# Stick-breaking attention: a third score bank, the scans' second operand and the column sums in one bank, filling output products in row order

## The chip, the cores and the metric

One core of one Trainium2 chip runs the kernel. The metric is the device time of one execution in microseconds (us), as the median of several executions. The engines are named as the profile names them: PE is TensorE (PEld its weight loads), DVE is VectorE, ACT is ScalarE, POOL is GpSimd and SP is SyncE, which issues most DMAs.

## What is computed

A decoder trunk of two layers on 1024 tokens with 1024 features. Layer 0 mixes tokens by a gated linear recurrence, layer 1 by stick-breaking attention with 16 heads of 64; a SwiGLU block follows each. The change lies in the attention alone. With z the scaled scores of a block of 128 queries against the keys up to them:

```python
strict = s_idx < t_idx
log_fail = jnp.where(strict, jax.nn.log_sigmoid(-z), 0.0)
suffix = lax.cumsum(log_fail, axis=3, reverse=True) - log_fail
weights = jnp.where(strict, jnp.exp(jax.nn.log_sigmoid(z) + suffix), 0.0)
outs.append(jnp.einsum("bhqk,bhkd->bhqd", weights.astype(vb.dtype), vb))
```

So a key's weight is its own sigmoid times the products of sigmoid(-z) over all keys between it and the query. Then the heads' outputs are multiplied by `attn_w_o` and added to the residual.

## The kernel before

**Products in 16-bit parts.** Most fp32 products are made as three fp16 products (`mm3`, lines 157 to 159: high x high, high x low, low x high). Rows in the profile with line 157, 158 or 159 are these.

**Pairs and chunks.** The 16 heads are worked in eight pairs q = 0 to 7 (`LAST` is 7). For each head, `chunk_list` gives twelve chunks of scores: eight with the diagonal (128 to 512 keys) and four more of 512 keys to their left for the later query blocks. A chunk passes through four steps:

- `z_part` (lines 2118, 2119): two TensorE products write the scores to a PSUM bank `z_ps`, from a pool `psZ` with two banks that are taken in turn.
- `z_rest` (line 2156): ScalarE takes the sigmoid of -z into SBUF (`w`; `wp`, `wd`, `wt` in the last pair).
- `scan` (lines 2164, 2167): a VectorE scan runs over the keys backwards and multiplies the sigmoids up. Its second operand holds 2^15 at the diagonal place and zeros elsewhere: it is fp32 in PSUM (`units_ps`), and for the last pair bfloat16 in SBUF (`unit`, read backwards). The scan of a left chunk starts from the first column of the diagonal chunk's result.
- `turn_weights` (lines 2179, 2180, 2189): ScalarE and GpSimd split the result into two fp16 parts, and a DMA transposes them. In the last pair TensorE transposes instead (`t_part`, line 2199), and ScalarE and VectorE split (`t_split`, lines 2208, 2209).

`av_part` (line 2231) multiplies the transposed weights with the differences of the values, eight to ten steps after the scores.

**PSUM.** Eight banks: two each for `psZ` (scores), `psT`, `psO` (weighted sums) and `psQ` (projections). Of `psT`, one bank holds `units_ps` until the last pair; the other serves `n_ps` of pair 0 and then stands unused until the last pair's transposes.

**Column sums.** For each pair, `column_norms` sums the squares of the value weights' columns: ScalarE squares them (`sq`, line 1968), eight one-column products form the sums on TensorE (`n_ps`, line 1950), and VectorE makes a power of two of them (lines 1956, 1958). For pairs 1 to 7, `n_ps` takes a bank of `psZ` in turn. `sums` is run by `due()`, which stands at the start of a step, before the step's `z_part`.

**The order.** All five engines keep the order in which the program is written (a manual schedule). The loop over `u` is the step: `due()`, then one chunk's `z_part` and `z_rest`, its `scan`, the previous chunk's `turn_weights`, one task from the list `later`, two filling projections (`fill`: six products for the next pair's q, k or v), and `av_part`. Semaphores are placed by the framework from the tiles that instructions touch.

**Filling output products.** In the last two heads there are no projections left, and `out_fill` starts the output projection: 21 rows of `mm3`, seven for each of three output tiles, at steps set by `amount`. Row k needs `xl[k]`, the heads of pair k; row 6 of each was third in order. `xl[6]` is written by lines 2255 and 2256 some steps after pair 6 is done.

**Set-up.** `unit` is made by GpSimd (lines 1913, 1914), and ScalarE casts it into `units_ps` (line 1916).

Of the kernel before, what the change touches and what calls it, by code (L numbers as in the profile page):

```python
# [8 lines left out]
F32 = mybir.dt.float32  # L9
F32R = mybir.dt.float32r  # L10
BF16 = mybir.dt.bfloat16
F16 = mybir.dt.float16
I32 = mybir.dt.int32
# [5 lines left out]
P = 128  # L19
S = 1024  # L20
D = 1024
ND = D // P
NT = S // P
NB = 512
# [11 lines left out]
def trunk(  # L36
# [21 lines left out]
    nc = tc.nc  # L58
# [33 lines left out]
    ident = cp.tile([P, P], F32, name="ident")  # L92
# [63 lines left out]
    def mm3(ps, wh, wl, mh, ml, first, last, **kw):  # L156
        nc.tensor.matmul(ps, lhsT=wh, rhs=mh, start=first, stop=False, **kw)  # L157
        nc.tensor.matmul(ps, lhsT=wh, rhs=ml, start=False, stop=False, **kw)  # L158
        nc.tensor.matmul(ps, lhsT=wl, rhs=mh, start=False, stop=last, **kw)  # L159

    def pair16(t):
        t = t.bitcast(F16)
        n = t.shape[-1] // 2
        return t[:, 0:n], t[:, n : 2 * n]
# [135 lines left out]
    with ExitStack() as st, tc.manual_schedule(engines={E.PE, E.Activation, E.DVE, E.Pool, E.SP}):  # L300
# [49 lines left out]
        ps = pst("vps0")  # L350
# [71 lines left out]
        for r0, r1 in ((0, 32), (32, 64), (64, P)):  # L422
            ps = pst("vps")
# [1475 lines left out]
    UP = 2.0**15  # L1899

    pos, obs, begun = ExitStack(), ExitStack(), {}
    with ExitStack() as st:
# [3 lines left out]
        psZ = pos.enter_context(tc.tile_pool(name="psZ", bufs=2, space=PSUM, side="right", reuse_waits="tile"))  # L1906
        psT = st.enter_context(tc.tile_pool(name="psT", bufs=2, space=PSUM, reuse_waits="tile"))
# [2 lines left out]


        unit = ap.tile([P, NB], BF16, name="unit")
        nc.gpsimd.memset(unit[:, 0 : NB - P], 0.0)
        nc.gpsimd.tensor_scalar_mul(unit[:, NB - P :], ident, UP)
        units_ps = psT.tile([P, NB], F32, tag="T", name="units")
        nc.scalar.copy(units_ps, unit[:, ::-1])
        g2 = ap.tile([P, ND], BF16, name="g2")
        nc.scalar.square(g2, vc[:, V_MIX + ND : V_MIX + 2 * ND])
        zz = ap.tile([P, NT], F32, name="zz")
# [12 lines left out]
        def stage(task, steps=1):  # L1932
            soon.append([steps, task])
# [8 lines left out]
        def column_norms(raw, q):  # L1942
            sq = ap.tile([P, ND, P], BF16, tag="vx", name="sq", bufs=2)
            r3 = raw.rearrange("p (k c) -> p k c", k=ND)

            def sums():
                pool, tag = (psZ, "z") if q else (psT, "T")
                n_ps = pool.tile([P, NB], F32, tag=tag, name="n_ps")[:, 0:1]
                for k in range(ND):
                    nc.tensor.matmul(  # L1950
                        n_ps, lhsT=sq[:, k], rhs=g2[:, k : k + 1], start=k == 0, stop=k == ND - 1
                    )

                n2, h = (ap.tile([P, 1], t, tag=x, name=x, bufs=2) for x, t in (("n2", F32), ("nh", I32)))
                sv[q], av_[q] = (ap.tile([P, 1], I32, tag=x, name=x, bufs=3) for x in ("sv", "av"))
                nc.vector.tensor_scalar(n2, n_ps, 1e-30, 2.0, op0=ALU.max, op1=ALU.mult)
                one = float(1 << 23)
                nc.vector.tensor_single_scalar(h, n2.bitcast(I32), 24, op=ALU.logical_shift_right)

                def factors():  # L1960
                    nc.gpsimd.tensor_scalar(sv[q], h, -one, 213 * one, op0=ALU.mult, op1=ALU.add)
                    nc.gpsimd.tensor_scalar(av_[q], h, one, 41 * one, op0=ALU.mult, op1=ALU.add)
                    nc.gpsimd.tensor_add(K_N, K_N, n2)
                    nc.gpsimd.tensor_mul(f32(av_[q]), f32(av_[q]), O_UP)

                stage(factors)

            squared = lambda i: nc.scalar.square(sq[:, 4 * i : 4 * i + 4], r3[:, 4 * i : 4 * i + 4])

            def second():  # L1970
                squared(1)
                stage(sums, 2)

            return lambda: squared(0), second
# [138 lines left out]

        def z_part(q, hx, j, ci, c0, c1, diag):
            nk = (j + 1) * P
            ps = psZ.tile([P, NB], F32, tag="z", name="z_ps")
            lhsT = Q[q][hx][:, j * P : (j + 1) * P]
            nc.tensor.matmul(ps[:, 0 : c1 - c0], lhsT=lhsT, rhs=KK[q][hx][:, 0, c0:c1], start=True, stop=False)
            nc.tensor.matmul(ps[:, 0 : c1 - c0], lhsT=lhsT, rhs=KK[q][hx][:, 1, c0:c1], start=False, stop=True)  # L2119
            return ps  # L2120
# [7 lines left out]
        LAST = NP - 1  # L2128
# [29 lines left out]
        def scan(q, hx, j, ci, c0, c1, diag):  # L2158
            F = W[q, hx, j, ci]
            n = min(c1, (j + 1) * P) - c0  # L2160
            rev = F[:, ::-1]
            add = unit[:, NB - n :][:, ::-1] if q == LAST else units_ps[:, 0:n]
            if diag:
                nc.vector.tensor_tensor_scan(rev, rev, add, 0.0, op0=ALU.mult, op1=ALU.add)  # L2164
            else:
                first = W[q, hx, j, 1][:, 0:1]
                nc.vector.tensor_tensor_scan(rev, rev, add, first, op0=ALU.mult, op1=ALU.bypass)

        T = {}
# [21 lines left out]
        def unit_list(q, hx):  # L2191
            kbs = ((0, 1, 2, 3), (4, 5, 6, 7, 0, 1, 2, 3))
            return [(q, hx, G, kb, kb == 4 * G, kb == 3) for G in range(2) for kb in kbs[G]]
# [70 lines left out]
        units = [u for q, hx in heads for u in unit_list(q, hx)]  # L2264
# [9 lines left out]
        def out_fill():  # L2274
            qs.close()
            po = obs.enter_context(tc.tile_pool(name="fp0", bufs=1, space=PSUM, side="right", reuse_waits="tile"))
            for x, n in ((0, 0), (0, 1), (1, 1)):
                d = mix[0].order[x]
                w = mix[0].w[d]
                if x:  # L2280
                    assert c >= len(chunks)
                    ps = psZ.tile([P, NB], F32, tag="z", name="ob_ps")
                else:
                    ps = po.tile([P, NB], F32, name=f"ob{n}")
                begun[d, n] = ps
                for k in (0, 1, 6, 2, 3, 4, 5):
                    mm3(ps, w[0][:, k], w[1][:, k], *pair16(xl[k][n]), k == 0, False)
                    yield

# [2 lines left out]
        with tc.manual_schedule(engines={E.PE, E.Activation, E.DVE, E.Pool, E.SP}):  # L2292
# [30 lines left out]
            gains = [len(units) - x for x in (31, 29, 27)]  # L2323

            last_two, out_work = len(units) - 2 * 12, out_fill()
            amount = {x: 2 for x in (9, 10, 11, 12)}
            amount.update({x: 1 for x in (*range(-5, 1), *range(14, 21))})
# [6 lines left out]
            for u in range(-LEAD, len(units)):  # L2334
# [6 lines left out]
                for a in some:  # L2341
                    z_rest(z_part(*a), *a)
# [5 lines left out]
                for a in some:  # L2348
                    scan(*a)
# [13 lines left out]
                if u in gains:  # L2363
                    z_rest(z_part(*chunks[c]), *chunks[c])
                    scan(*chunks[c])
                    turning.append(chunks[c])
                    c += 1
# [52 lines left out]
```

## Time and profile before

| | |
|---|---|
| median of 3 runs | 2058.79 us (2058.74 to 2060.89) |
| profiled execution | 2058.67 us, its span 2056.2 us |
| PE busy | 2008.2 us (98%) |
| DVE busy | 1778.6 us (86%) |
| ACT busy | 1451.3 us (71%) |
| POOL busy | 297.6 us (14%) |
| granted TensorE clock | 1.00 |
| first and last score product | 972.0 and 1342.0 us |

The span runs from the first to the last instruction; the execution's time is 2.5 us longer. Times in rows are counted from the span's start. A row of the timeline gives start, duration, engine, line, operation, the tile written and the tiles read, the shape and the count; in brackets, the idle time of the engine just before and what ended it. A row of a list of waits gives who waited for whom, the total in us, how often and the longest. TensorE's products overlap: the next one starts some 0.22 us after one of 512 columns began, though each lasts 0.38.

### The profile page before, as it was taken

How to read it: one execution, taken by the hardware profiler on the slowest of the kernel's cores; microseconds unless marked ns; L12 is line 12 of the kernel's file. 1: busy time of each engine (PE TensorE's matmuls, PEld its weight loads, DVE VectorE, ACT ScalarE, POOL GpSimd, SP SyncE). 2: the span in 40 equal slices, each digit the busy share in tenths (PEclk: the TensorE clock that was granted, in tenths of full speed). 3: DMA queues.
4: the chain of work that ended last, by engine and by line, in shares of the span. 5: the costliest groups of instructions: out<-in, count | busy, mean ns of one | idle time of the engine just before them, and what ended most of it. 6: DMA issues, size and time to landing. Idle time of an engine off the chain costs nothing. (4 is left out here: it accounts for less than half of the span.)

```text
span 2056.2 us, 28572 instructions
## 1 busy us (share of the span) xinstructions
PE 2008.2 (98%) x10059; PEld 1095.0 (53%) x10059; DVE 1778.6 (86%) x2639; ACT 1451.3 (71%) x2280; POOL 297.6 (14%) x327
## 2 busy tenths in 40 slices
PE   8999999999999999999999999899999999999998
PEld 7888885454555444444545445454445555444445
DVE  6887888989999899897888877878899999999886
ACT  6777546777777677766888888854768777665566
POOL 1000010000000000001666666412000000000002
PEclk9999999999999999999999999999999999999999
DMA  7232471564555797523888887554355556674412
GB/s 257 62 93 62 147 242 62 159 213 161 179 176 188 247 298 223 161 90 93 151 157 154 147 152 155 116 177 152 114 178 186 168 164 214 211 258 146 134 42 92
DMA packets 443999, 328.07 MB, mean 160 GB/s; under 512 B 165832, under 2 KB 365648, under 8 KB 443856
## 3 DMA queue, kind: packets, MB, share of 16 engines
q1 hardware_dynamic: 443696, 325.99, 55.0%
q8 instruction: 78, 1.28, 0.3%
q14 instruction: 65, 0.53, 0.1%
q10 hardware_dynamic: 160, 0.27, 0.0%
HBM read 215.55 MB, written 69.21 MB: 138 GB/s over the span
## 5 line engine op out<-in xcount | busy, mean ns | idle before, releaser
L159 PE MATMUL p_ps<-v,wb 128*128 128x512 f16 x524 | 198.7, 379 | 3.8 <-DVE wb L785 3.4
L159 PE MATMUL p_ps<-v,wc 128*128 128x512 f16 x524 | 198.6, 379 | 3.2 <-DVE wc L785 3.2
L157 PE MATMUL p_ps<-v,wb 128*128 128x512 f16 x524 | 198.5, 379 | 2.9 <-ACT ta L1487 0.8
L158 PE MATMUL p_ps<-v,wc 128*128 128x512 f16 x524 | 198.6, 379 | 0.0
L158 PE MATMUL p_ps<-v,wb 128*128 128x512 f16 x524 | 198.6, 379 | 0.0
L157 PE MATMUL p_ps<-v,wc 128*128 128x512 f16 x524 | 198.5, 379 | 0.0
L2180 POOL TENSOR_TENSOR wx<-w,wx 128x512 f16<-128x512 f32 (+1 forms) x140 | 153.1, 1095 | 119.8 <-ACT wx L2179 85.6
L159 PE MATMUL p_ps<-v,wa 128*128 128x512 f16 x396 | 150.1, 379 | 0.0
L158 PE MATMUL p_ps<-v,wa 128*128 128x512 f16 x396 | 150.1, 379 | 0.0
L157 PE MATMUL p_ps<-v,wa 128*128 128x512 f16 x396 | 150.0, 379 | 0.0
L780 ACT ACTIVATE wb<-sb,fac 128x1024 f16<-128x1024 f32 x44 | 50.5, 1148 | 110.4 <-DVE sb L800 110.4
L2164 DVE TENSOR_TENSOR_SCAN w<-w,units 128x128 f32<-128x128 f32 (+1 forms) x112 | 91.3, 815 | 39.7 <-ACT w L2156 39.6
L245 POOL TENSOR_TENSOR acc<-acc,rbc 128x512 f32<-128x512 f32 x30 | 39.6, 1321 | 495.9 <-ACT rbc L244 495.8
L157 PE MATMUL p_ps<-v,wd 128*128 128x512 f16 x254 | 96.2, 379 | 8.3 <-ACT G L1487 4.7
L2156 ACT ACTIVATE w<-z_ps,zz 128x512 f32<-128x512 f32 (+2 forms) x168 | 95.5, 576 | 8.6 <-PE z_ps L2119 6.9
L158 PE MATMUL qk_ps<-rh,w 128*128 128x512 f16 x264 | 100.0, 379 | 0.3 <-DVE rh L251 0.3
L159 PE MATMUL qk_ps<-rh,w 128*128 128x512 f16 x264 | 100.0, 379 | 0.0
L157 PE MATMUL qk_ps<-rh,w 128*128 128x512 f16 x264 | 100.0, 379 | 0.0
L157 PE MATMUL a_ps<-xh,whi 128*128 128x512 f32 x248 | 97.1, 391 | 0.0
L159 PE MATMUL p_ps<-v,wd 128*128 128x512 f16 x254 | 96.3, 379 | 0.8 <-DVE wd L785 0.8
L2179 ACT CAST wx<-w 128x512 f16<-128x512 f32 (+1 forms) x140 | 79.8, 570 | 24.4 <-DVE w L2164 13.2
L158 PE MATMUL a_ps<-xl,whi 128*128 128x512 f32 x248 | 96.6, 390 | 0.1
(493 smaller groups left out, 5621.5 us busy)
## 6 DMA issues: line engine op xcount, KB each, us to landing
raw<-in_ffn_w_in SPq DMA_DIRECT2D x80, 512.0 KB, 4.3
pd<-U SPq DMA_DIRECT2D x90, 256.0 KB, 2.4
loose<-in_ffn_w_out SPq DMA_DIRECT2D x44, 512.0 KB, 3.7
raw<-pd SPq DMA_DIRECT2D x66, 256.0 KB, 3.6
row<-pd SPq DMA_DIRECT2D x62, 256.0 KB, 4.5
raw<-in_ffn_w_out SPq DMA_DIRECT2D x56, 256.0 KB, 3.8
raw<-in_attn_w_qkv SPq DMA_DIRECT2D x24, 512.0 KB, 4.2
raw<-in_lru_w_out SPq DMA_DIRECT2D x16, 512.0 KB, 3.6
```

Of the source, the lines that this page charges most:

```text
L157: nc.tensor.matmul(ps, lhsT=wh, rhs=mh, start=first, stop=False, **kw)
L158: nc.tensor.matmul(ps, lhsT=wh, rhs=ml, start=False, stop=False, **kw)
L159: nc.tensor.matmul(ps, lhsT=wl, rhs=mh, start=False, stop=last, **kw)
L245: (eng or nc.gpsimd).tensor_add(acc[n], acc[n], sq)
L780: nc.scalar.activation(h, r, AF.Copy, scale=up)
L2156: nc.scalar.activation(F, ps[:, 0:n], AF.Sigmoid, scale=zs)
L2164: nc.vector.tensor_tensor_scan(rev, rev, add, 0.0, op0=ALU.mult, op1=ALU.add)
L2179: nc.scalar.copy(wx[:, 0:m, 0], F)
L2180: nc.gpsimd.tensor_sub(wx[:, 0:m, 1], F, wx[:, 0:m, 0])
```

## The change

Four things are altered, in three functions and the set-up. The scans' second operand for pairs 0 to 6 becomes bfloat16 and so takes half of its bank; the copy is made by VectorE as 256 32-bit words, and `unit` is laid out forwards from the start. The other half of that bank takes the column sums, one column for each pair. The second `psT` bank becomes `zx`, a third bank for scores, which every third chunk uses in pairs 0 to 6. The filling output products take rows 0 to 6 in order.

```diff
         unit = ap.tile([P, NB], BF16, name="unit")
-        nc.gpsimd.memset(unit[:, 0 : NB - P], 0.0)
-        nc.gpsimd.tensor_scalar_mul(unit[:, NB - P :], ident, UP)
-        units_ps = psT.tile([P, NB], F32, tag="T", name="units")
-        nc.scalar.copy(units_ps, unit[:, ::-1])
+        nc.gpsimd.memset(unit[:, P:], 0.0)
+        nc.gpsimd.tensor_scalar_mul(unit[:, 0:P], ident[:, ::-1], UP)
+        both_ps = psT.tile([P, NB], F32, tag="T", name="units")
+        units_ps, norm_ps = both_ps[:, 0 : NB // 2].bitcast(BF16), both_ps[:, NB // 2 :]
+        nc.vector.tensor_copy(both_ps[:, 0 : NB // 2].bitcast(I32), unit.bitcast(I32))
+        zx, z_at = psT.tile([P, NB], F32, tag="T", name="zx"), [0]
...
             def sums():
-                pool, tag = (psZ, "z") if q else (psT, "T")
-                n_ps = pool.tile([P, NB], F32, tag=tag, name="n_ps")[:, 0:1]
+                n_ps = norm_ps[:, q : q + 1]
...
         def z_part(q, hx, j, ci, c0, c1, diag):
             nk = (j + 1) * P
-            ps = psZ.tile([P, NB], F32, tag="z", name="z_ps")
+            z_at[0] += 1
+            ps = zx if z_at[0] % 3 == 0 and q != LAST else psZ.tile([P, NB], F32, tag="z", name="z_ps")
...
-            add = unit[:, NB - n :][:, ::-1] if q == LAST else units_ps[:, 0:n]
+            add = (unit if q == LAST else units_ps)[:, 0:n]
...
-                for k in (0, 1, 6, 2, 3, 4, 5):
+                for k in range(ND - 1):
                     mm3(ps, w[0][:, k], w[1][:, k], *pair16(xl[k][n]), k == 0, False)
```

## The prediction

> **What bounds the kernel now.** I read the page's busy shares first, then the busy times of the attention stage, then what TensorE waited for, then single rows around the steps that the change touches.
>
> ```profile
> span 2056.2 us, 28572 instructions
> PE 2008.2 (98%) x10059; PEld 1095.0 (53%) x10059; DVE 1778.6 (86%) x2639; ACT 1451.3 (71%) x2280; POOL 297.6 (14%) x327
> ...
> 1220.00:1270.00 50.00, 48.87 (x275) 25.20 (x274) 40.73 (x51) 42.11 (x78) 33.29 (x35) 1.00 0.77 152
> 1309.00:1347.00 38.00, 31.68 (x186) 18.09 (x186) 37.84 (x49) 26.70 (x51) 11.32 (x7) 1.00 0.24 49
> ```
>
> The last two rows are stretches of the attention stage; the columns are start and end, length, then busy time (instructions) of TensorE, its weight loads, VectorE, ScalarE and GpSimd, then clock, DMA share and GB/s. While pairs 0 to 6 are scored (the first stretch is typical) TensorE is the bound, 48.87 of 50 us, and what it idles is time of the kernel. In the last pair (the second stretch) the bound is VectorE, 37.84 of 38 us, and TensorE has 6.3 us to spare. The clock is full in both. The two stretches must be costed by different rules: in the first a TensorE wait counts in full, in the second only VectorE's own time does.
>
> ```profile
> PE z_ps L2118 <- ACT w L2156: 8.4, 14, 1.0
> PE ob L158 <- DVE rl L2256: 1.9, 1, 1.9
> PE z_ps L2118 <- ACT w L2156: 7.1, 12, 0.8
> 985.55 0.38 PE L2118 MATMUL z_ps<-kk,q 128*128 128x512 f16 x1 [0.38 <-ACT w L2156]
> ```
>
> These are TensorE's waits: the first two rows over the whole span, the third between 999 and 1308 us, and the first single wait of the kind. A score product waits for the sigmoid that empties its bank: 14 times, 8.4 us. One output product waits 1.9 us for the row that it multiplies. These two are all that the change can win.
>
> **The third bank.** With two banks a score product needs the sigmoid two products back to be over, with three the sigmoid three back. Every wait above is under 1 us and products are some 2 us apart, so one bank more takes away all of them in pairs 0 to 6: the one of 0.38 us and the twelve with 7.1 us. Where that leads depends on the next part.
>
> **The column sums move into the scans' bank.** Each pair needs eight one-column products (`n_ps`, L1950). Before, they took a score bank in turn; now they write column 256+q of the tile whose first half is the scans' second operand. TensorE would then write a bank that VectorE's scans read. Does the program let the two overlap? The kernel before shows how two engines on one tile's bank are ordered:
>
> ```profile
> DVE hc L364 <- ACT xh L360: 10.4, 6, 5.2
> 26.43 1.27 ACT L360 ACTIVATE xh<-tp,g 128x512 fp32r<-128x512 f32 x2 [0.28 <-PE tp L357]
> 27.15 0.69 DVE L364 COPY hc<-tp 128x512 f32<-128x512 f32 x1 [0.18 <-ACT xh L360]
> ```
>
> The copy `hc<-tp` reads only `tp`, which TensorE finished before 26.43; it uses nothing of `xh`. It still starts only when ScalarE's read of the same bank ends (two in 1.27 us: the first at some 27.07), six times, 10.4 us. Even two readers of a bank are kept apart. I take it that a writer is kept from a reader as well, also at other columns of the bank.
> The Trainium skill (PSUM — Partial Sum Buffer, PSUM bank collisions raise a hardware error) says that two different engines may not be on one bank and the same partitions at once, disjoint columns or not, and that accesses are to be guarded by bank. By that rule the sum is the one below; without it, it is that of the first rival. The trace agrees with the rule in the six waits above; no row shows the case of disjoint columns.
>
> So `n_ps` waits for the scan issued just before it, that of the last score product. Rows at the sums of pair 1, pair 2 and pair 7:
>
> ```profile
> 1004.19 0.34 PE L1950 MATMUL n_ps<-g,sq 128*128 128x1 bf16 x8
> 1004.36 0.95 DVE L2164 TENSOR_TENSOR_SCAN w<-w,units 128x384 f32<-128x384 f32 x1 [0.30 <-ACT w L2156]
> 1004.39 0.38 PE L2118 MATMUL z_ps<-kk,q 128*128 128x512 f16 x1
> ...
> 1053.53 0.38 PE L2118 MATMUL z_ps<-kk,q 128*128 128x512 f16 x1
> 1055.69 0.34 PE L1950 MATMUL n_ps<-g,sq 128*128 128x1 bf16 x8
> 1055.70 0.69 ACT L2156 ACTIVATE w<-z_ps,zz 128x512 f32<-128x512 f32 x1
> 1056.44 0.38 PE L2118 MATMUL z_ps<-kk,q 128*128 128x512 f16 x1 [0.41 <-ACT w L2156]
> 1056.48 1.28 DVE L2167 TENSOR_TENSOR_SCAN w<-w,w,units 128x512 f32<-128x512 f32 x1 [0.86 <-ACT w L2156]
> ...
> 1299.83 0.38 PE L2118 MATMUL z_ps<-kk,q 128*128 128x512 f16 x1 [0.41 <-ACT w L2156]
> 1299.87 1.28 DVE L2167 TENSOR_TENSOR_SCAN w<-w,w,units 128x512 f32<-128x512 f32 x1 [0.87 <-ACT w L2156]
> ...
> 950.27 0.69 DVE L1805 TENSOR_TENSOR rbc<-rbc,acc 128x512 f32<-128x512 f32 x1
> 951.02 1.05 PE L232 MATMUL st_ps<-ones,rbc 128*128 128x1 f32 x8 [0.65 <-DVE rbc L1805]
> ```
>
> From VectorE's end to TensorE's start takes 0.06 us (950.96 to 951.02), and the eight products cost 0.20 us when nothing follows late (1004.19 to 1004.39). At pair 2 the next score product started at 1056.44, when the sigmoid was over, and the scan began 0.04 later and took 1.28. Now it starts at 1056.48 + 1.28 + 0.06 + 0.20 = 1058.02: 1.58 us later, the old wait of 0.41 included. Pairs 2 to 7 all show this picture (the last rows are pair 7), each 1.58. Pair 1 has a shorter scan and no old wait: 1004.36 + 0.95 + 0.26 - 1004.39 = 1.18 us. Queued behind the waiting `n_ps` on TensorE are the score product, the six filling products and the weighted sums of the step; ScalarE, which began the sigmoid of 1055.70 1.6 us after its product (1053.53 to 1054.13) was there, does not notice. VectorE's next scan waits for `n_ps` too, but it needs the score product behind it anyway. For pair 0 no scan has begun.
>
> The waits that the third bank takes away besides, in the same stretch:
>
> ```profile
> 1068.97 0.38 PE L2118 MATMUL z_ps<-kk,q 128*128 128x512 f16 x1 [0.69 <-ACT w L2156]
> ...
> 1197.46 0.38 PE L2118 MATMUL z_ps<-kk,q 128*128 128x512 f16 x1 [0.29 <-ACT w L2156]
> ...
> 1264.05 0.38 PE L2118 MATMUL z_ps<-kk,q 128*128 128x512 f16 x1 [0.68 <-ACT w L2156]
> 1083.43 0.69 ACT L2156 ACTIVATE w<-z_ps,zz 128x512 f32<-128x512 f32 x1 [0.70 <-PE z_ps L2119]
> ```
>
> The first and the last of five, 0.68 to 0.69 each, some 13 us after the sums of pairs 2 to 6: 3.42 us; the single 0.29; and the 0.38 at 985.55. The other six of the twelve are those right behind `n_ps`, already in the 1.58. The last row shows ScalarE waiting for TensorE once per pair: there it catches up, so each pair starts afresh and the terms add.
>
> **Pair 7 and after.** The sums of pair 7 come at 1299 us, when ScalarE is behind:
>
> ```profile
> 1302.82 0.69 ACT L2156 ACTIVATE w<-z_ps,zz 128x512 f32<-128x512 f32 x1
> 1304.15 0.38 PE L2118 MATMUL z_ps<-kk,q 128*128 128x512 f16 x1
> 1308.25 0.69 ACT L2156 ACTIVATE w<-z_ps,zz 128x512 f32<-128x512 f32 x1
> 1308.97 1.28 DVE L2167 TENSOR_TENSOR_SCAN w<-w,w,units 128x512 f32<-128x512 f32 x1 [0.39 <-ACT w L2156]
> DVE w L2167 <- ACT w L2156: 0.4, 1, 0.4
> ```
>
> The product of 1299.83 is read at 1302.82, that of 1304.15 at 1308.25; 1.58 us later, both are still in time. From 1309 to 1347 VectorE waits once, 0.4 us (last row, that stretch). So pair 7's stall is hidden: I take 0, with 1.58 as the other end. The same cover makes **the rows in order** worth nothing: row 6 comes last instead of third, the 1.9 us wait for it goes, and as many products stand at each step; but it lies at 1321, inside the stretch that VectorE sets, and the next thing late is again a product behind VectorE's split or scan. I take 0; a gain of 1.9 is the other end. The score wait of 1.0 us in pair 7 is treated likewise.
>
> **The operand itself.** Scans now read bfloat16 in PSUM instead of fp32. The nearest rows on both sides:
>
> ```profile
> L2167 DVE TENSOR_TENSOR_SCAN w<-w,w,units 128x512 f32<-128x512 f32 x56 | 71.4, 1276 | 22.8 <-ACT w L2156 20.9 <-POOL two L2087 1.9
> L2167 DVE TENSOR_TENSOR_SCAN wt<-wt,wp,unit 128x512 f32<-128x512 f32 x4 | 5.0, 1260 | 0.0
> ```
>
> fp32 in PSUM 1276 ns, bfloat16 in SBUF 1260: neither place nor type matters by over 0.02 us. In the first stretch VectorE has 9 us of 50 to spare; only the scans ahead of `n_ps` count, 6 x 0.02. I take 0, ends -0.1 and +0.1. The last pair's scans read the same operand forwards; its place and type are those of the second row: 0. Setting up:
>
> ```profile
> 951.55 0.54 POOL L1914 TENSOR_SCALAR unit<-ident 128x128 bf16<-128x128 f32 x1
> 952.88 0.58 ACT L1916 CAST units<-unit 128x512 f32<-128x512 bf16 x1
> 952.41 0.16 DVE L207 TENSOR_SCALAR rs_m<-st_ps 128x4 f32<-128x4 f32 x1 [1.44 <-ACT rs_s L206]
> 955.82 1.05 PE L217 MATMUL rb_ps<-ident,rcol 128*128 128x128 f32 x8
> ```
>
> ScalarE's 0.58 us cast becomes a VectorE copy of half as many words, which must wait for GpSimd's row (over at 952.09) while VectorE idles 1.44 us anyway; TensorE comes for the factors only at 955.82. GpSimd reads the identity backwards, at most another 0.54. No DMA moves and no queue is passed. 0.
>
> **The sum**, against the profiled run's own 2058.67 us (span 2056.2; the median of the runs is 2058.79, 0.1 above): -0.38 + 1.18 + 5 x 1.58 - 3.42 - 0.29 = +5.0. 2058.67 + 5.0 = 2063.7 us.
>
> **Rivals.** (1) *Faster: the sums do not wait.* If only overlapping columns are ordered, `n_ps` passes at once and the third bank's gain stands alone: -0.38 - 7.07 + 0.41 (pair 7, hidden) = -7.0, 2051.6 us. It decides if `n_ps` starts before the running scan ends. Against it: the `hc` rows. (2) *No change: ScalarE closes up.* If ScalarE is less behind at the sums, being fed later and held less, the scan ends earlier. Of the wait 0.68 us less per pair would leave 5.0 - 5 x 0.68 = +1.6, 2060.3 us. For it: those 1.6 us behind at 1055.70 are slack that could close; against it: ScalarE's own instructions ahead of it come in a fixed burst.
>
> (3) *Slower still: TensorE runs ahead and waits longer at the sums.* If a wait taken away only lengthens the next stall, the credits vanish: 1.18 + 7.90 = 9.1, 2067.8 us, and 2069.3 with pair 7 exposed. Against it: the 0.70 at 1083.43.
>
> **Chances and range.** Forecast 0.56, rival 1 0.10, rival 2 0.24, rival 3 0.10. About 0.2% (4.1 us) can be told from no change: below 2054.7 is faster, above 2062.9 slower. The forecast's own range is 2061.8 (row 6 counts) to 2065.3 (pair 7 counts), some 7 in 10 of it above the bound: slower 0.56 x 0.7 + 0.10 = 0.49 to 0.52; same the rest with rival 2, 0.38; faster 0.10. The range leaves out rival 1 and the upper part of rival 3: 2058.0 to 2067.5.
>
> **What would show it.** TensorE waits of some 2 us at `n_ps`, put down to VectorE's scans, seven of them, 13 to 16 us in all; no score wait on sigmoids between 972 and 1308; the wait of `ob` for `rl` gone and waits on VectorE's splits longer; the stretch after pair 6 as long as before. If `n_ps` shows no wait, rival 1 is right; if the waits are there but half as long, rival 2.

## The result and the profile after

The changed kernel takes 2067.25 us (median of five, 2066.11 to 2069.93), the kernel before on the same chip 2059.45 (2058.74 to 2060.89): ratio 1.004, 95% interval 1.0025 to 1.0054, so 7.8 us slower. The profiled execution is one of the longer ones, 2069.23 us with a span of 2067.5.

First the totals on the page of the changed kernel, and its TensorE waits from 990 to 1360 us (who waited for whom, total in us, times, longest):

```profile
span 2067.5 us, 28572 instructions
PE 2013.0 (97%) x10059; PEld 1094.7 (53%) x10059; DVE 1779.3 (86%) x2640; ACT 1451.3 (70%) x2279; POOL 298.4 (14%) x327
...
PE units L1951 <- DVE w L2169: 12.8, 6, 3.0
PE av_ps L2233 <- DVE wx L2211: 4.0, 4, 1.3
PE z_ps L2120 <- ACT wd L2158: 1.0, 2, 0.7
PE units L1951 <- DVE w L2166: 0.8, 1, 0.8
```

The column sums are now written to the tile `units`. They wait for the scans, seven times, 13.6 us. The score waits of pairs 0 to 6 are gone, and so is the wait of `ob` for `rl`; the waits on VectorE's split in the last pair are longer (3.1 us before). All of this was forecast. But TensorE also got 4.8 us busier with the same instructions (2008.2 before), which was not. The timeline at the sums of pairs 2, 3 and 7 (start, duration, work; in brackets idle time before and what ended it):

```profile
1056.35 0.38 PE L159 MATMUL qk_ps<-xg,w 128*128 128x512 f16 x1
1057.41 1.28 DVE L2169 TENSOR_TENSOR_SCAN w<-w,w,units 128x512 f32<-128x512 f32 x1 [0.86 <-ACT w L2158]
1058.74 0.34 PE L1951 MATMUL units<-g,sq 128*128 128x1 bf16 x8 [2.01 <-DVE w L2169]
1058.94 0.38 PE L2120 MATMUL z_ps<-kk,q 128*128 128x512 f16 x1
...
1107.13 0.38 PE L159 MATMUL qk_ps<-xg,w 128*128 128x512 f16 x1
1109.29 0.34 PE L1951 MATMUL units<-g,sq 128*128 128x1 bf16 x8 [1.78 <-DVE w L2169]
...
1258.13 0.38 PE L159 MATMUL qk_ps<-xg,w 128*128 128x512 f16 x1
1260.34 0.34 PE L1951 MATMUL units<-g,sq 128*128 128x1 bf16 x8 [1.83 <-DVE w L2169]
...
1310.09 1.28 DVE L2169 TENSOR_TENSOR_SCAN w<-w,w,units 128x512 f32<-128x512 f32 x1 [0.86 <-ACT w L2158]
1311.42 0.34 PE L1951 MATMUL units<-g,sq 128*128 128x1 bf16 x8 [2.32 <-DVE w L2169]
1311.62 0.38 PE L2120 MATMUL z_ps<-kk,q 128*128 128x512 f16 x1
```

The scan ends at 1057.41 + 1.28 = 1058.69 and the sums start 0.05 later: they wait for it to the end, though it reads other columns. What follows the stall is seen in stretches of one window each (start and end, length, busy time (instructions) of TensorE, its weight loads, VectorE, ScalarE, GpSimd, then the granted clock, DMA share, GB/s):

```profile
1060.20:1063.60 3.40, 3.40 (x11) 1.42 (x10) 2.24 (x2) 1.66 (x4) 2.22 (x6) 0.51 1.01 228
1107.90:1111.30 3.40, 2.02 (x17) 1.07 (x17) 1.95 (x4) 3.36 (x7) 2.27 (x2) 1.00 0.66 163
1159.20:1162.60 3.40, 3.28 (x16) 1.34 (x16) 1.60 (x5) 2.75 (x5) 2.29 (x3) 0.51 1.52 211
1210.40:1213.80 3.40, 3.40 (x10) 1.24 (x9) 2.29 (x3) 1.99 (x4) 2.48 (x3) 0.51 1.16 197
1261.60:1265.00 3.40, 3.40 (x10) 1.29 (x9) 2.23 (x2) 1.45 (x4) 2.41 (x6) 0.51 0.96 238
1312.80:1316.20 3.40, 3.40 (x11) 1.35 (x10) 1.28 (x1) 3.03 (x6) 1.94 (x3) 0.51 1.22 299
```

After five of the seven stalls (pairs 2, 4, 5, 6 and 7) the granted clock is half for 3.4 us, which costs 1.7 us of TensorE work each time; after that of pair 3 (second row) it stays full. In the stage before, it was full throughout. Last come 300 us of the stage in both kernels, before and then after, and the last pair after:

```profile
1000.00:1300.00 300.00, 292.69 (x1637) 150.21 (x1635) 240.21 (x296) 254.94 (x473) 197.38 (x204) 1.00 0.82 153
```

```profile
1000.00:1300.00 300.00, 288.14 (x1581) 146.59 (x1580) 235.10 (x288) 245.45 (x454) 191.18 (x197) 0.98 0.79 149
...
1319.00:1357.00 38.00, 33.04 (x200) 19.10 (x199) 37.45 (x50) 27.26 (x52) 10.68 (x7) 1.00 0.24 49
```

The last pair is as before, VectorE full, 10 us later. All that is lost is lost before it. Pair by pair, from one first score product behind the sums to the next (start to start in the timelines):

| pairs | before, us | after, us | stall at its end | half clock within |
|---|---|---|---|---|
| 2 to 3 | 48.32 | 50.54 | 1.78 | yes |
| 3 to 4 | 49.00 | 50.05 | 2.95 | no |
| 4 to 5 | 49.41 | 50.41 | 1.87 | yes |
| 5 to 6 | 48.35 | 50.60 | 1.83 | yes |
| 6 to 7 | 48.31 | 51.08 | 2.32 | yes |

Every row of after is, within 0.2 us, 46.9 + its stall + 1.7 where the clock was halved (50.4, 49.9, 50.5, 50.4, 50.9). The 46.9 is fitted here; the runs below find it again. The pair from 3 to 4 is nearly as long at full clock, because its stall is the longest, 2.95 us; why it is longer was not looked into. From this table alone, then, half clock could merely take the place of a longer stall. `e2_shared_bank_alone` and `e10_filled_same_order` below decide that.

### The profile page after: what moved, and what is told of

Its sections match the earlier page's. It is cut to its first block, busy times and chain, and to the rows that moved or that the text cites. A ratio compares the mean times of both kernels' runs of the same rounds, so it can differ in the third digit from the quotient of the medians.

```text
span 2067.5 us, 28572 instructions
## 1 busy us (share of the span) xinstructions
PE 2013.0 (97%) x10059; PEld 1094.7 (53%) x10059; DVE 1779.3 (86%) x2640; ACT 1451.3 (70%) x2279; POOL 298.4 (14%) x327
## 4 chain that ended last, share of the span: by engine, by line
PE 33%; DVE 8%; ACT 5%; issue 2%; DMA 1%; POOL 1%; DVEq 0%; ACTq 0%; POOLq 0%
PE p_ps L159 7%; PE p_ps L157 6%; PE p_ps L158 6%; PE qk_ps L159 2%; PE qk_ps L158 2%; PE qk_ps L157 2%; PE av_ps L2233 2%; DMA wd<-wx 1%; PE ob_ps L157 1%; PE ob_ps L159 1%; PE ob_ps L158 1%; DVE v L1395 1%; ACT w L2158 1%; DVE w L2169 1%; POOL wx L2182 1%
## 5 line engine op out<-in xcount | busy, mean ns | idle before, releaser
L780 ACT ACTIVATE wb<-sb,fac 128x1024 f16<-128x1024 f32 x44 | 50.5, 1148 | 109.9 <-DVE sb L800 109.9
L2169 DVE TENSOR_TENSOR_SCAN w<-w,w,units 128x512 f32<-128x512 f32 x56 | 71.4, 1276 | 29.7 <-ACT w L2158 25.1
L159 PE MATMUL a_ps<-xh,wlo 128*128 128x512 f32 x248 | 96.6, 389 | 0.0
```

The lines of the kernel that those rows point to most:

```text
L780: nc.scalar.activation(h, r, AF.Copy, scale=up)
```

## The experiments

Theory A: the stalls cost what was forecast, and the clock adds its own term. Rival B: the excess comes from the third bank, the row order or the new operand. Then a second question: is TensorE the bound of pairs 0 to 6, so that its waits are time? Each ratio is to the kernel before on the same chip.

### Which part of the change

`e1_sums_apart`: the whole change, but the sums of pairs 1 to 7 take a score bank in turn, as before.

```diff
-                n_ps = norm_ps[:, q : q + 1]
+                n_ps = score_bank(q - 1)[:, 0:1] if q else norm_ps[:, 0:1]
...
```

The lines left out move the choice of the bank from `z_part` into `score_bank`.

> The changed kernel, but the column sums of pairs 1 to 7 take a score bank in turn (two of the pool and zx), as the scores do; the bank with the scans' operand is written by TensorE for pair 0 alone. Theory A (the sums wait for the scan that reads their bank, and the stretches of half TensorE clock follow from that stall): no wait on scans, no half-speed stretch between 1000 and 1300 us, granted clock 1.00 there, and the third bank's gain alone: -7.0, 2051 to 2053 us, ratio 0.9965. Theory B (the bfloat16 operand, the third bank or the order of the rows costs the time or the clock): still 2062 us or more, with half-speed stretches.

Measured: 2058.91 against 2058.93 us, ratio 1.000 (0.9991 to 1.0009). The whole loss belongs to the shared bank. And the third bank's gain, expected at 7.0 us, does not come. The TensorE waits and two of ScalarE's of this kernel, 1000 to 1300 us:

```profile
PE z_ps L1951 <- ACT sq L1969: 4.4, 3, 1.6
PE zx L1951 <- ACT sq L1969: 2.8, 2, 1.6
...
ACT wx L2184 <- DVE w L2169: 12.5, 18, 1.6
ACT wx L2184 <- DMA wp<-wx: 7.2, 5, 1.8
```

The 7.1 us of score waits have come back as 7.2 us at the sums, now for ScalarE's squares, and ScalarE waits longer for the buffers that the transposing DMA empties (2.1 us before).

`e2_shared_bank_alone`: the whole change with two score banks and the old order of rows.

```diff
...
-            ps = zx if z_at[0] % 3 == 0 and q != LAST else psZ.tile([P, NB], F32, tag="z", name="z_ps")
+            ps = psZ.tile([P, NB], F32, tag="z", name="z_ps")
...
-                for k in range(ND - 1):
+                for k in (0, 1, 6, 2, 3, 4, 5):
```

> The changed kernel with two score banks and the old order of the rows: only the operand's half bank and the column sums beside it are left of the change. Theory A: six to seven waits of 1 to 3 us of the sums on scans, half-speed stretches behind some of them, and because TensorE is held there the waits for sigmoids mostly go without a third bank: 2065 to 2069 us, as the whole change. If the third bank is worth its 3.4 us also beside the stalls: 2069 to 2072. Theory B (third bank or rows to blame): 2059.

Measured: 2065.93 against 2058.93, ratio 1.0038 (1.0025 to 1.005), with four stretches at half clock. The shared bank alone makes the loss; rival B falls. This run also prices the clock by itself. Two of its pairs, 3 to 4 and 5 to 6, each end with a stall of 1.8 us, and only the second has a stretch at half clock (span of the pair, length, the busy times as above, then the clock):

```profile
1108.99:1157.84 48.85, 47.08 (x271) 24.23 (x267) 39.30 (x48) 41.11 (x77) 32.08 (x34) 1.00 0.81 151
...
1208.87:1259.41 50.54, 48.77 (x271) 24.69 (x268) 39.39 (x48) 41.14 (x77) 32.17 (x34) 0.97 0.81 147
```

It is 1.69 us longer, and TensorE is 1.69 us busier with the same products.

`e3_rows_alone`: the kernel before with the rows in order.

```diff
-                for k in (0, 1, 6, 2, 3, 4, 5):
+                for k in range(ND - 1):
```

> The kernel before with the filling output products in row order, and nothing else. Theory A (the last pair's stretch is VectorE's): the wait of 1.9 us of the output product for row 6 goes, the waits on VectorE's splits behind it grow, 2059 us, ratio 1.000. If that wait was on the path: 2057.

Measured: 2060.38 against 2060.22, ratio 1.0002 (0.9993 to 1.001). The wait for `rl` goes and nothing comes of it.

### What a stall costs, with and without the clock

`e4z_score_first`, `e5_stall_half`, `e4_stall_filled`: the changed kernel with the step's score product ahead of the sums, made once, three and six times (the repeats write the same values). For pairs 1 to 7 `sums` only puts its work on the list `sums_due`, and `z_part` runs it (shown for six times).

```diff
...
+            for _ in range(6 if sums_due else 1):
                 nc.tensor.matmul(ps[:, 0 : c1 - c0], lhsT=lhsT, rhs=KK[q][hx][:, 0, c0:c1], start=True, stop=False)
                 nc.tensor.matmul(ps[:, 0 : c1 - c0], lhsT=lhsT, rhs=KK[q][hx][:, 1, c0:c1], start=False, stop=True)
+            while sums_due:
+                sums_due.pop(0)()
```

> The changed kernel, but in the steps with column sums the score product (once) goes ahead of the sums: 0.43 us of the stall is used, nothing is added. Gaps of 1.3 to 1.7 us are left at the sums. If half speed needs about 1.7 us of idle time within one 3.4 us stretch, it is gone or rare (clock 0.998 or more), and the stalls fit into what TensorE has to spare: 2058 to 2060 us. If gaps of 1.4 us set it off too: clock 0.995 to 0.997 and 2064 us or more.

> As the kernel with the stall filled, but the score product is issued three times, 1.3 us: a gap of 0.8 to 1.2 us is left at the sums. The changed kernel's trace shows half speed after gaps of 1.8 us and more that lie within one 3.4 us stretch, and none after a gap split into 0.5 and 1.3. Theory A: gaps, but no half-speed stretch; the score product is out of the stall, so 0.43 us per pair less than with six: about 2061 to 2062 us. If any gap sets off half speed: clock 0.995 and 2065 or more.

> The changed kernel, but in the steps with column sums the score product goes ahead of the sums and is issued six times over (the last counts), 2.6 us of TensorE work where it stood idle. The sums still wait for the scan. Theory A: TensorE has no idle gap over 1 us there, so no half-speed stretch, granted clock 1.00; the stall's own cost stays: +5, about 2064 us against 2067 of the change. Theory C (the half-speed stretches come by themselves, or cost nothing): clock 0.995 to 0.997 and 2067 us.

Measured: once, 2059.2 against 2060.22, ratio 0.9998 (0.9989 to 1.0006); three times, 2058.77 against 2058.93, 0.9998 (0.9989 to 1.0006); six times, 2061.86 against 2058.93, 1.0014 (1.0004 to 1.0023). The last two are 2 to 3 us faster than was expected. TensorE's waits in the first (1000 to 1300 us), then the stretch in the first and in the last:

```profile
PE units L1958 <- DVE w L2179: 9.2, 6, 1.8
PE units L1958 <- DVE w L2176: 1.0, 1, 1.0
```

```profile
1000.00:1300.00 300.00, 289.81 (x1623) 148.63 (x1622) 240.46 (x294) 254.52 (x472) 197.24 (x203) 1.00 0.81 152
```

```profile
1000.00:1300.00 300.00, 299.84 (x1673) 153.80 (x1671) 239.62 (x293) 251.63 (x467) 196.61 (x203) 1.00 0.78 152
```

In the first, stalls of 1.5 us per pair at the sums are left and the clock stays full: it costs nothing. In the last, 2.15 us of products per pair (ten more, some 0.215 us apart) stand in the stall's place, TensorE never idles, and only 2.9 us are lost in all, about 0.5 per pair. So TensorE has some 1.6 us of room in each pair: it is not the bound. A pair takes 49.08 us in that timeline; less the 2.15 us this is 46.9 again.

`e10_filled_same_order`: the order of the changed kernel kept, sums first; four dummies of the coming score product fill the wait.

```diff
...
+            while sums_due:
+                for _ in range(4):
+                    nc.tensor.matmul(ps[:, 0 : c1 - c0], lhsT=lhsT, rhs=KK[q][hx][:, 0, c0:c1], start=True, stop=False)
+                    nc.tensor.matmul(ps[:, 0 : c1 - c0], lhsT=lhsT, rhs=KK[q][hx][:, 1, c0:c1], start=False, stop=True)
+                sums_due.pop(0)()
```

> The changed kernel with its order kept (the sums wait for the scan, and the score product stands behind them), but ahead of the sums TensorE issues the coming score product four times over into its bank, 1.7 us of work that the real product overwrites. So the stall is the same and TensorE is busy in most of it. Theory F (the half-speed stretches are what the change costs beyond some 3 us): clock 0.998 or more, 2061 to 2063 us. Theory G (the cost is the loop that the change closes: scan, sums, next score product, next sigmoid, so that ScalarE starves behind the sums; half speed only takes the place of a longer stall): 2065 to 2067 us at full clock.

Measured: 2062.21 against 2059.75, ratio 1.0009 (1.0 to 1.0018).

```profile
1000.00:1300.00 300.00, 299.18 (x1665) 153.00 (x1664) 239.66 (x294) 253.01 (x468) 196.53 (x202) 1.00 0.80 152
```

The score product comes as late as in the changed kernel (0.25 us after the scan's end in pairs 2 to 7 of both), but TensorE is kept busy and the clock stays full: 2.5 us slower instead of 7.8. The difference, some 5 us, is the clock. Theory A's second half stands; its first does not, as the stalls by themselves cost 2.5 us and not the 5.0 that were forecast.

`e6_sums_late`: the sums behind the step's filling products, and that step's scan behind the sums.

```diff
...
-                for a in some:
+                for a in some if not sums_due else ():
                     scan(*a)
...
+                if sums_due:
+                    sums_due.pop(0)()
+                    for a in some:
+                        scan(*a)
```

> The changed kernel with the sums still in the scans' bank, but issued after the step's filling products, and the step's scan behind them: TensorE comes to the sums when the scan before is about over. Theory D (ScalarE with its transposing DMAs sets some 48.4 us per pair, TensorE has about 1.5 us per pair to spare, which is where the third bank's gain went): no wait of 0.5 us or more at the sums, clock as before, and still 2057 to 2060 us. Theory E (TensorE is the bound, what it waits is lost): all its waits of the stage gone, 2050 to 2053 us.

Measured: 2058.73 against 2060.22, ratio 0.9992 (0.9983 to 1.0), three stretches at half clock in the profiled run. Theory D expected no wait of 0.5 us or more at the sums; of 13.6 us in seven, 5.6 in four are left, and two of these, of 1.9 and 2.1 us, have half clock behind them. The kernel is where the one before is, as what is left fits about into TensorE's room. That the third bank gains can't be told from this.

### Why the third bank gains nothing

`e7_apart_squares_early`: `e1_sums_apart` with both halves of the squares one step earlier, so that the sums need not wait for them.

```diff
...
-            def second():
+            def both():
+                squared(0)
                 squared(1)
-                stage(sums, 2)
...
-            return lambda: squared(0), second
+            return both, lambda: stage(sums, 2)
...
```

> The kernel with the sums in the score banks (three of them), and both halves of the squares taken by ScalarE one step earlier, so that the sums find them done. Theory D: the waits of the sums for the squares (7.2 us in five) go, and the time comes back as other waits, ScalarE's for a split buffer that a DMA still reads above all: 2056 to 2060 us. Theory E: 2050 to 2052 us.

Measured: 2059.76 against 2060.22, ratio 0.9997 (0.9988 to 1.0006). The waits for squares go and TensorE waits elsewhere (from 1000 to 1300 us, 3.5 us for sigmoids and 1.8 us for the transposing DMAs): the pace is set by something behind it.

`e11_copies_dve` moves two of ScalarE's copies per chunk of projections onto VectorE in the kernel before, `e12_banks_copies_dve` does it in `e7_apart_squares_early`.

```diff
-                    nc.scalar.copy(KK[q][hx][a, x, cs], two[a, x])
+                    (nc.vector.tensor_copy if x else nc.scalar.copy)(KK[q][hx][a, x, cs], two[a, x])
...
-                    nc.scalar.copy(Q[q][hx][a, cs], two[a, 0])
+                    nc.vector.tensor_copy(Q[q][hx][a, cs], two[a, 0])
```

> The kernel before, with half of ScalarE's copies of q and k (lines 2076 for the low part and 2084) made by VectorE: some 3 to 4 us per pair less on ScalarE. Theory D (ScalarE's chain sets 48.4 us per pair, TensorE needs 46.9): 48.4 falls towards 47, six pairs, 2050 to 2055 us. If TensorE, the DMAs or VectorE set the pace: 2058 to 2062 us.

> The kernel with three score banks, the sums in them and the squares early, and the same copies made by VectorE. Theory D: now TensorE's 46.9 us per pair is what is left, the third bank keeps it fed: 2049 to 2053 us. If transposing DMAs hold ScalarE's split buffers (that wait was 7.2 us with three banks): 2055 to 2059 us.

Measured: 2073.72 and 2070.9 against 2059.75, ratios 1.0069 (1.0056 to 1.0081) and 1.0056 (1.0042 to 1.007), slower where a gain was expected. The stretch and ScalarE's longest waits in `e11_copies_dve`:

```profile
1000.00:1300.00 300.00, 281.36 (x1570) 143.74 (x1568) 258.28 (x333) 216.10 (x401) 190.38 (x196) 1.00 0.78 147
...
ACT wx L2179 <- DVE w L2167: 31.3, 14, 2.8
ACT wx L2179 <- DVE w L2164: 26.3, 25, 2.2
```

ScalarE got 39 us lighter in 300 and the kernel 14 us longer: ScalarE's splits wait for scans, which now come behind copies. Sigmoid (ScalarE), scan (VectorE) and split (ScalarE) of successive chunks hand over to each other, and load on either side lengthens the round. The second kernel is 2.8 us faster than the first, which the two intervals can't tell from nothing.

`e14_no_squares` and `e13_banks_no_squares`: ScalarE squares the weights for pair 0 only, and the other pairs take pair 0's sums (the scale factors of pairs 1 to 7 are left out); two instructions of 0.63 us on ScalarE per pair go, with the buffer that they wrote, and nothing takes their place. The first is otherwise the kernel before, the second `e1_sums_apart`.

```diff
...
-            squared = lambda i: nc.scalar.square(sq[:, 4 * i : 4 * i + 4], r3[:, 4 * i : 4 * i + 4])
+            squared = lambda i: None if q else nc.scalar.square(sq[:, 4 * i : 4 * i + 4], r3[:, 4 * i : 4 * i + 4])
...
```

> The kernel before with the same squares left out. If the third bank is worth nothing by itself: the same time as the three banks without squares, 2050 to 2054 us. If the third bank pays once ScalarE has time to spare: this one at 2055 to 2058 us, the other some 3 to 5 us faster.

> The kernel with three score banks and the sums in them, but ScalarE squares the value weights of pair 0 only; the sums of the other pairs use those squares again (so their scale factors are pair 0's). This takes 1.25 us per pair off ScalarE and puts it nowhere. If the chain through ScalarE (and the scans that it waits for) sets the 48.4 us per pair: some 47.2 us per pair, 2050 to 2054 us. If VectorE alone or the DMAs set it: 2057 to 2060 us.

Measured: 2053.25 and 2052.64 against 2059.28, ratios 0.9972 (0.9962 to 0.9983) and 0.9967 (0.9954 to 0.9979). The stretch in the first and in the second:

```profile
1000.00:1300.00 300.00, 297.82 (x1672) 153.03 (x1670) 243.94 (x300) 254.54 (x470) 202.25 (x209) 1.00 0.81 158
```

```profile
1000.00:1300.00 300.00, 299.41 (x1680) 153.53 (x1679) 243.42 (x300) 254.21 (x471) 202.73 (x209) 1.00 0.82 158
```

Relieving ScalarE gives 6.0 us with two banks: the score waits shrink, to 2.2 us in five, without any third bank. Only in the second is TensorE full (299.41 of 300), and there a pair takes 46.9 to 47.3 us in its timeline, from the 46.9 of the table up. The third bank is worth 0.6 us beside it, which these intervals can't tell from nothing.

`e15_squares_pool` and `e16_banks_squares_pool`: the whole computation, with the squares of pairs 1 to 7 on GpSimd; the first is otherwise the kernel before, the second `e7_apart_squares_early`.

```diff
+            def squared(i):
+                x = r3[:, 4 * i : 4 * i + 4]
+                if q:
+                    nc.gpsimd.tensor_mul(sq[:, 4 * i : 4 * i + 4], x, x)
+                else:
+                    nc.scalar.square(sq[:, 4 * i : 4 * i + 4], x)
```

> The kernel before with the squares of pairs 1 to 7 computed on GpSimd instead of ScalarE; all else as before. If ScalarE's load sets the pace of pairs 0 to 6, the 6 us of the run without squares come here too: 2052 to 2055 us. If GpSimd's own work, which the squares lengthen, then holds back what follows them, the gain is lost or turns into a loss: 2058 us or more, and ScalarE's or VectorE's waits on GpSimd grow.

> The three-bank kernel whose column sums take score banks (no shared bank), with the squares of pairs 1 to 7 one step earlier and on GpSimd. If ScalarE's load alone sets the pace, 2051 to 2054 us, at most 1 us under the run with the same squares and the banks of before; if the third bank is worth its 7 us once ScalarE is relieved, 2046 to 2049; if GpSimd then holds back what follows, 2058 or more.

Measured: 2054.56 and 2053.3 against 2059.01, ratios 0.998 (0.9971 to 0.9989) and 0.9974 (0.9964 to 0.9985). Both are faster than either kernel. The stretch of the first, with its one group of TensorE waits above 1 us, then the stretch of the second:

```profile
1000.00:1300.00 300.00, 295.95 (x1657) 151.93 (x1656) 242.38 (x298) 252.97 (x466) 214.23 (x221) 1.00 0.82 156
...
PE n_ps L1950 <- POOL sq L1971: 3.7, 7, 1.1
```

```profile
1000.00:1300.00 300.00, 296.74 (x1659) 151.90 (x1658) 242.07 (x300) 251.41 (x467) 214.13 (x220) 1.00 0.82 155
```

GpSimd had the time (197 of 300 us busy before, 214 now), and most of what ScalarE's squares cost is won: 4.5 and 5.7 of some 6 us. The second, with the third bank and the squares a step earlier, is 1.3 us ahead by the medians, within the intervals of each other.

## Why the prediction was right or wrong

The direction and the place were right, the size too small: +5.0 was forecast, +7.8 measured. 2067.25 lies above the forecast's own range (2061.8 to 2065.3) and just inside the wide one (to 2067.5). That it lies there is luck. Without the clock, for which the sum has no term, the same stalls cost 2.5 us (`e10_filled_same_order`), half of what was forecast for them.

- **The sums wait for the scan: right, near to the tenth at first.** Pair 2's score product was put at 1056.44 - 0.38 + 1.18 + 1.58 = 1058.82; it starts at 1058.94. By the Trainium skill (PSUM — Partial Sum Buffer, PSUM bank collisions raise a hardware error) two engines are to be kept off one bank at once, at disjoint columns too; the trace agrees, as the program keeps the two apart, 13.6 us in seven waits. Whether the chip would have stood for the overlap, no run here shows.
- **"The clock is full in both": this step failed.** It was read from the kernel before and carried over to the one after. The terms of the sum held no price for what a stall does to the clock: 1.7 us of TensorE work for each of five. Four of these lie in the pairs of the table and count in full; the fifth comes behind pair 7's product, where part of the delay is covered. With the stalls filled, 2.5 us of the 7.8 are left.
- **"What it idles is time of the kernel", "a TensorE wait counts in full": this failed too.** TensorE's work in a pair is 46.9 us (the fit and `e13_banks_no_squares`), the pace of an undisturbed pair 48.3 (three of five rows of the table). The 7.1 us of score waits were this room, not a cost: the third bank took them away for 0.0 us (interval -1.9 to +1.9 us) where rival 1 had -7.0. For the same reason a stall of 1.5 us per pair costs nothing (`e4z_score_first`). The credits of 3.42 us did not exist, and neither did most of the debits of 1.58; in the sum the two errors hid each other.
- **Rivals 1 and 2** fall on the waits at the sums, which are neither absent nor half as long.
- **Rival 3** (waits taken away lengthen the next ones) has a time near the measured one, 2067.8 us, but not its sum: 9.1 us of longer waits. The waits at the sums are as long as forecast, 13.6 us in seven within the 13 to 16; what was wrong is what they cost.
- **Pair 7's stall, the row order, the last pair, the operand and the set-up at 0: right.** The scan ahead of pair 7's sums starts 10.2 us late (1299.87, now 1310.09), and the last pair is still 10 us late with VectorE full; row order alone measures 1.0002; the long scans take 1.28 us as before; the first score product starts at 972.0 us in both.

Put right, the sum for the profiled execution is: 2.5 us up to pair 2's product; five pairs at 46.9 + stall, and 1.7 more in the four with a halved clock, which together take 252.68 instead of 243.39 us, 9.3 more. Of these 11.8 at pair 7's product 1.2 is covered behind it: the execution was 10.6 longer (2069.23 against 2058.67). The median run has a clock of 0.997 where this one has 0.995, so fewer halved stretches. What makes the pairs from 3 to 5 of the kernel before 0.7 to 1.1 us longer than their neighbours was not looked into.

## What to carry to other kernels

A wait that comes back every round on an engine that is 97% busy may be its room and not its cost: before pricing it in full, ask whether the engine it waits for is in a round of its own (here sigmoid, scan, split) that would be no shorter without the wait, and take load off that round first. Where one PSUM bank is shared by the writer and the reader of different columns, as here, the program's semaphores put the two in sequence; place such a product behind other work of its engine. And price a stall of TensorE of 2 us twice: for itself, and for the clock after it.

## What the runs showed of the hardware

The granted clock falls for 3.41 us after idle times of about 2 us. The halved stretches start at 1060.1, 1159.1, 1210.3, 1261.5 and 1312.7 us, 29 or 15 times 3.413 apart: they lie on one grid, though the stalls do not. An idle time of 1.83 us (1258.5 to 1260.3), which lies in one interval of that grid (1258.1 to 1261.5), was enough; that of 1.78 us ahead of 1109.3 is cut by the grid at 1107.9 into 0.4 and 1.4 and had no effect. In `e2_shared_bank_alone` one of 1.77 us within an interval, ahead of 1308.1, was enough: the clock is half from 1308.9. The Trainium skill (TensorE: Matmul & The Clock Gate, HAM oscillation — how this bites in real kernels) gives as its rule no idle gaps over some 3.4 us. The trace agrees with a window of that length, at half clock, but not with the gap: by the rule the stalls here, 2.95 us at most, would have left the clock alone, and five stretches at half clock followed them. The measurement decides: somewhat over half a window is enough here.
